# Cross-covariance attention: the V side moved later, with V loads and stores alternating in the closing part

## The chip, the cores and the metric

The kernel runs on one core of one Trainium2 chip. The metric is device time in microseconds (us) of one execution, taken as the median over runs. Times inside an execution are counted from the start of the profiled span.

## The reference

Q, K and V are float32 of shape (8, 12, 512, 64): 96 heads of 512 rows by 64 columns. Each column of Q and K is divided by its norm over the 512 rows. The attention matrix is 64 x 64 for each head, not 512 x 512:

```python
attn = np.einsum('bhnd,bhne->bhde', Q_norm, K_norm)
attn = np.exp(attn - np.max(attn, axis=-1, keepdims=True))
attn = attn / (np.sum(attn, axis=-1, keepdims=True) + 1e-10)
return np.einsum('bhnd,bhde->bhne', V, attn)
```

So every byte of Q, K and V is read once and the output, as large as V, is written once.

## The kernel before

Four heads make a unit, so there are 24 units (U = 24, numbers 0 to 23). One unit of Q, K, V or output is 512 KB and travels as one DMA. All DMAs are issued by SP in program order: 24 loads each of Q, K and V, and 24 stores, the last of them split into two halves of 256 KB. The order of work on every engine is written out by hand (`manual_schedule`), and each engine takes its instructions strictly in that order.

The attention side of a unit s runs as follows. DVE casts Q and K to bf16 (`cast_q` line 80, `cast_k` line 83). PE forms the gram matrices in 32 matmuls (`grams`, line 96). DVE reads the squared norms off the diagonals (`norms`, line 111), POOL raises them to the power -0.5 (line 116) and scales K's half of the gram (`scale_k`, line 121), which ACT had copied out of PSUM (`keep_kq`, line 104). PE transposes (`logits`, line 127), DVE scales by Q's norm (`scale_q`, line 131), ACT takes the exponential (`exps`, line 135), and DVE divides by the sum (`normalise`, lines 139 to 143). The finished matrix of unit u goes into a buffer of `abuf`, chosen by u modulo the number of buffers; PE and ACT then put a second copy into its lower half (`doubled`, lines 160 and 161). The zeros of these buffers are written once, at the start, by POOL (line 194).

The V side of a unit is a cast to bf16 (`cast_v`, line 87, on ACT in the loop and on DVE in the closing part), eight transposes on PE and their copy to SBUF on ACT (`vtrans`, lines 153 and 155), and sixteen matmuls with two copies out of PSUM (`outs`, lines 171 and 175). In the loop both copies are ACT's. In the closing part, from the unit after n1 on, one of them is DVE's.

One loop runs over s = 0 to 23. `outs_by(s)` says how many units of V have their outputs by the end of step s. In step s, SP gets the loads of Q and K of unit s + 3, then loads of V up to unit n1 + 3 and stores up to unit n1 - 4, where n1 = outs_by(s). Before the change outs_by(s) = (s - 2) * 10 // 11, so that n1 is 19 in the last step: the loop leaves the outputs of five units, one V load and eight stores to the closing part.

Buffers limit how early things can start: five for Q and for K, six for the float32 V (`vp`), four for the bf16 V, three for the transposed V, ten for the outputs, two PSUM tiles each for the grams (`ps_g`, which the closing part's `vtrans` also uses) and for the outputs.

The closing part begins after the loop with `logits(last)`. There the attention of the last unit is completed, and the outputs of the remaining units follow.

Of the kernel before, what the change touches and what calls it, by code (L numbers as in the profile page):

```python
# [23 lines left out]
def kernel(  # L24
# [7 lines left out]
    nc = tc.nc  # L32
    B, H, N, _ = Q.shape
    assert N == MV * R and Q.shape[3] == D
    U = B * H // HU
# [21 lines left out]

    def outs_by(s):

        return max(0, (s - 2) * 10 // 11)  # L60


    qf, kf, vf, vb, qkb, gram, nsq, rq, kqs, sl, ex, vt, so, kq = ({} for _ in range(14))
# [7 lines left out]
    def load_v(u):  # L71
        vf[u] = vp.tile([128, SV, TP * 2 * D], F32, name="vf")
        nc.sync.dma_start(out=vf[u], in_=Vf[u])

    def store(u, g=slice(0, SV)):
        nc.sync.dma_start(out=Of[u][:, g], in_=so[u][:, g].rearrange("p s t d -> p s (t d)"))
# [8 lines left out]
    def cast_v(u, copy=nc.scalar.copy):  # L85
        w = vb[u] = vbp.tile([128, SV, TP, 2 * D], BF16, name="vb")
        copy(w.rearrange("p s t d -> p s (t d)"), vf[u])  # L87
# [37 lines left out]
    def logits(u):  # L125
        for h in range(HU):
            nc.tensor.transpose(lg[:, h, :], kqs[u][D:, h, :], ident[D:, D:])  # L127

    def scale_q(u):
        s = sl[u] = small.tile([D, HU, D], F32, name="sl")  # L130
        nc.vector.tensor_tensor(out=s, in0=lg, in1=rq[u][0:D, :, None].to_broadcast([D, HU, D]), op=ALU.mult)  # L131
# [5 lines left out]
    def normalise(u):  # L137
        s = small.tile([D, HU], F32, name="esum")
        nc.vector.reduce_sum(out=s, in_=ex[u], axis=AX.X)  # L139
        ri = small.tile([D, HU], F32, name="rinv")  # L140
        nc.vector.reciprocal(ri, s)
        a = abuf[u % len(abuf)]
        nc.vector.tensor_tensor(out=a[0:D, :, 0, :], in0=ex[u], in1=ri[:, :, None].to_broadcast([D, HU, D]), op=ALU.mult)  # L143

    def vtrans(u, spare=False):

        if not spare:
            ps = ps_v.tile([128, SV, TP, 128], BF16, name="vps")
        else:
            ps = ps_g.tile([128, 2, 512], F32, name="gram")[:, 0].bitcast(BF16).rearrange("p (s t c) -> p s t c", s=SV, t=TP)  # L150
        for g in range(SV):
            for t in range(TP):
                nc.tensor.transpose(ps[:, g, t, :], vb[u][:, g, t, :], identb)  # L153
        w = vt[u] = vtp.tile([128, SV, TP, 128], BF16, name="vt")
        nc.scalar.copy(w, ps)  # L155

    def doubled(u):

        a = abuf[u % len(abuf)]
        nc.tensor.matmul(dup[D:], identb[0:D, 0:D], a[0:D, :, 0, :], tile_position=(0, D))  # L160
        nc.scalar.copy(a[D:, :, 1, :], dup[D:])  # L161

    def outs(u, copies=(nc.scalar.copy, nc.scalar.copy)):
        s = so[u] = sop.tile([128, SV, TP, 2 * D], F32, name="so")
        a = abuf[u % len(abuf)]
        for g in range(SV):
            po = ps_o.tile([128, TP, 2 * D], F32, name="po")
            for t in range(TP):
                for x in range(2):
                    rows = slice(MV * x, MV * (x + 1))  # L170
                    nc.tensor.matmul(  # L171
                        po[rows, t, :], vt[u][:, g, t, rows],
                        a[:, 2 * g + x].rearrange("p a d -> p (a d)"), tile_position=(0, MV * x),
                    )
            copies[g](s[:, g], po)  # L175
# [13 lines left out]
    mhalf = const.tile([128, HU], F32, name="mhalf")  # L189
    nc.gpsimd.memset(mhalf, -0.5)  # L190
    abuf = []
    for i in range(9):
        a = const.tile([128, HU, 2, D], BF16, name=f"ab{i}")
        nc.gpsimd.memset(a, 0.0)
        abuf.append(a)

    def on(f, u):
        if 0 <= u < U:
            f(u)
# [5 lines left out]
    nv, nst, nt = 2, 0, 0  # L205
    for s in range(U):
        n0, n1 = outs_by(s - 1), outs_by(s)
        on(load_qk, s + LOAD_AHEAD)
        while nv < min(U, n1 + 4):
            load_v(nv)  # L210
            nv += 1
        while nst < n1 - 3:
            store(nst)
            nst += 1
        new = range(nt, n1 + 1) if s >= 1 else ()
        for v in new:
            cast_v(v)
        on(cast_q, s + 1)
        on(normalise, s - 2)
        on(grams, s)  # L220
        on(norms, s)
        on(keep_kq, s)
        on(scale_k, s)
        on(logits, s - 1)
        on(scale_q, s - 1)
        on(exps, s - 1)
        on(cast_k, s + 1)
        for v in range(n0, n1):
            outs(v)
        on(doubled, s - 2)  # L230
        for v in new:
            vtrans(v)
            nt = v + 1
    for u in range(nv, U):
        load_v(u)
    for u in range(nst, U):
        if u >= n1:
            break
        store(u)
        nst += 1  # L240


    last = U - 1
    both = (nc.scalar.copy, nc.vector.tensor_copy)
    logits(last)
    cast_v(n1 + 1, nc.vector.tensor_copy)
    normalise(last - 1)
    scale_q(last)
    exps(last)
    outs(n1)  # L250
    store(n1)
    vtrans(n1 + 1, True)
    doubled(last - 1)
    normalise(last)
    doubled(last)
    cast_v(n1 + 2, nc.vector.tensor_copy)
    for u in range(n1 + 1, U):
        if u + 1 < U:
            vtrans(u + 1, True)
        if u + 2 < U:  # L260
            cast_v(u + 2, nc.vector.tensor_copy)
        outs(u, both)
        if u < last:
            store(u)
    for g in range(SV):
        store(last, slice(g, g + 1))

# [29 lines left out]
```

## Time and profile before

| what | value |
|---|---|
| median of 7 runs | 136.63 us (135.52 to 137.26) |
| the profiled execution's own time | 137.26 us |
| its span | 135.5 us |
| moved by the hardware DMA queue | 50.34 MB, mean of all queues 373 GB/s |
| PE busy | 87.5 us (65%) |
| DVE busy | 89.8 us (66%) |
| ACT busy | 96.0 us (71%) |
| POOL busy | 64.3 us (47%) |
| mean granted TensorE clock | 0.836 |

The span runs from the first to the last instruction; the execution's own time is 1.76 us longer. The profiled execution is the slowest of the seven, 0.63 us above their median. The busy times are means over a loop and a closing part which differ much, so no engine's share tells by itself what sets the end.

### The profile page before, as it was taken

The page shows a single profiled execution, that of the slowest core. Times are in us where ns is not written, and L with a number is a line of the kernel's source. Part 1 is how long each engine was busy: PE and PEld are TensorE (multiplying, and loading weights), DVE is VectorE, ACT ScalarE, POOL GpSimd, SP SyncE. Part 2 cuts the span into 40 slices and gives each one's busy share as a digit, 9 for nine tenths or more (in the row PEclk, how much of TensorE's full clock was granted, in tenths as well). Part 3 has the DMA queues.
Part 4 walks back from the last instruction along what each step waited for, and adds up shares of the span by engine and source line. Part 5 has one row for each costly group of instructions (what it writes and reads, how often), then busy time and mean ns, then how long its engine had stood idle before and what let it go on. Part 6 is the DMA issues. An engine that isn't in the chain of part 4 may idle for free.

```text
span 135.5 us, 3877 instructions
## 1 busy us (share of the span) xinstructions
PE 87.5 (65%) x1464; PEld 69.4 (51%) x1464; DVE 89.8 (66%) x344; ACT 96.0 (71%) x161; POOL 64.3 (47%) x65
## 2 busy tenths in 40 slices
PE   0056854397677696785965595868955388976940
PEld 0046733275455474564853484647744266654730
DVE  0755662989988888878684859776482766843540
ACT  3002730549999999999997397999978488986760
POOL 8705641478678638564276337642642426510000
PEclk9999999999999959999599559995599955555595
DMA  4999999999999999999999999999999999997475
GB/s 125 377 391 389 387 387 388 386 384 386 385 386 386 406 405 395 405 397 397 402 396 402 406 391 400 403 400 404 402 400 402 408 409 399 406 402 287 161 269 221
DMA packets 26146, 50.58 MB, mean 373 GB/s; under 512 B 1552, under 2 KB 1552, under 8 KB 26128
## 3 DMA queue, kind: packets, MB, share of 16 engines
q1 hardware_dynamic: 26128, 50.34, 98.5%
q8 instruction: 11, 0.18, 0.5%
q14 instruction: 7, 0.06, 0.1%
HBM read 37.75 MB, written 12.58 MB: 371 GB/s over the span
## 4 chain that ended last, share of the span: by engine, by line
DMA 54%; ACT 14%; PE 12%; DVE 12%; issue 3%; SPq 1%; ACTq 0%; DVEq 0%
DMA qf<-in_Q_dram 54%; DVE scr L111 4%; PE gram L96 4%; ACT so L175 4%; ACT vt L155 4%; PE po L171 3%; PE gram L153 3%; ACT vb L87 2%; DVE qkb L80 2%; ACT ab L161 2%; ACT ex L135 1%; PE vps L153 1%; DVE sl L131 1%; ACT kq L104 1%; DVE so L175 1%
## 5 line engine op out<-in xcount | busy, mean ns | idle before, releaser
L116 POOL TENSOR_TENSOR rq<-nsq,mhalf 128x4 f32<-128x4 f32 x24 | 44.3, 1847 | 51.6 <-DVE nsq L111 39.0
L96 PE MATMUL gram<-qkb 64*128 64x128 bf16 x768 | 35.1, 261 | 9.6 <-DVE qkb L83 9.6
L96 PEld LDWEIGHTS <-qkb 64*128 64x128 bf16 x768 | 29.9, 117 | 19.6 <-DVE qkb L83 17.1
L80 DVE CAST qkb<-qf 128x1024 bf16<-128x1024 f32 x24 | 18.1, 752 | 22.8 <-DMA qf<-in_Q_dram 22.7
L104 ACT COPY kq<-gram 64x256 f32<-64x256 f32 x24 | 8.8, 368 | 26.5 <-DVE nsq L111 26.2
L111 DVE CUSTOM_DVE_ANT_0 scr<-gram,ident 128x128 f32<-128x128 f32 x96 | 21.9, 279 | 5.7 <-PE gram L96 5.7
L175 ACT COPY so<-po 128x512 f32<-128x512 f32 x44 | 23.8, 589 | 0.7 <-PE po L171 0.2
L171 PE MATMUL po<-ab,vt 128*64 128x128 bf16 x384 | 19.0, 255 | 6.5 <-ACT vt L155 5.6
L87 ACT CAST vb<-vf 128x1024 bf16<-128x1024 f32 x20 | 21.0, 1048 | 2.7 <-DMA vf<-in_V_dram 2.7
L153 PEld LDWEIGHTS <-vb 128*128 128x128 bf16 x192 | 14.0, 116 | 16.0 <-ACT kq L104 9.4
L155 ACT COPY vt<-vps 128x1024 bf16<-128x1024 bf16 x20 | 20.2, 1012 | 0.7 <-PE vps L153 0.3
L171 PEld LDWEIGHTS <-vt 128*64 128x64 bf16 x384 | 14.7, 131 | 10.6 <-ACT vt L155 8.9
L127 PE MATMUL lgdup<-ident,kqs 64*64 64x64 f32 x96 | 12.2, 264 | 9.8 <-POOL kqs L121 5.1
L160 PE MATMUL lgdup<-ab,identb 64*64 64x256 bf16 x24 | 7.5, 314 | 15.6 <-DVE sl L131 14.3
L83 DVE CAST qkb<-kf 128x1024 bf16<-128x1024 f32 x24 | 16.2, 675 | 0.0
L153 PE MATMUL vps<-identb,vb 128*128 128x128 bf16 x160 | 15.0, 249 | 1.8 <-ACT vb L87 1.2
L121 POOL TENSOR_TENSOR kqs<-kq,rq 64x256 f32<-64x256 f32 x24 | 14.8, 617 | 2.4 <-POOL rq L116 0.6
L127 PEld LDWEIGHTS lgdup<-ident,kqs 64*64 64x64 f32 x96 | 8.4, 136 | 12.4 <-POOL kqs L121 9.4
L131 DVE TENSOR_TENSOR sl<-lgdup,rq 64x256 f32<-64x256 f32 x24 | 9.9, 413 | 3.1 <-PE lgdup L127 2.4
L139 DVE TENSOR_REDUCE esum<-ex 64x4 f32<-64x256 f32 x24 | 9.8, 406 | 3.3 <-ACT ex L135 3.2
L143 DVE TENSOR_TENSOR ab<-ex,rinv 64x256 bf16<-64x256 f32 x24 | 10.7, 445 | 0.8
L135 ACT ACTIVATE ex<-sl 64x256 f32<-64x256 f32 x24 | 10.0, 417 | 0.9 <-DVE sl L131 0.3
(18 smaller groups left out, 43.2 us busy)
## 6 DMA issues: line engine op xcount, KB each, us to landing
qf<-in_Q_dram SPq DMA_DIRECT2D x24, 512.0 KB, 10.4
kf<-in_K_dram SPq DMA_DIRECT2D x24, 512.0 KB, 10.4
vf<-in_V_dram SPq DMA_DIRECT2D x24, 512.0 KB, 10.3
out_dram<-so SPq DMA_DIRECT2D x23, 512.0 KB, 10.2
out_dram<-so SPq DMA_DIRECT2D x2, 256.0 KB, 2.8
```

What stands on the lines that cost most here:

```text
L80: nc.vector.tensor_copy(qkb[u][:, :, :, 0:D], qf[u].rearrange("p s (t d) -> p s t d", d=D))
L83: nc.vector.tensor_copy(qkb[u][:, :, :, D:], kf[u].rearrange("p s (t d) -> p s t d", d=D))
L87: copy(w.rearrange("p s t d -> p s (t d)"), vf[u])
L96: nc.tensor.matmul(g[:, c, 2 * D * p:2 * D * (p + 1)], x, x, start=(t == 0), stop=(t == R - 1), tile_position=(MV * c, 0),)
L111: nc.vector.tensor_tensor_reduce(out=scr, in0=gram[u][:, h % 2, 2 * D * (h // 2):2 * D * (h // 2 + 1)], in1=ident, scale=1.0, scalar=1e-20 ...
L116: nc.gpsimd.tensor_tensor(out=r, in0=n2, in1=mhalf, op=ALU.pow)
L121: nc.gpsimd.tensor_tensor(out=kk[D:], in0=kq[u][D:], in1=rq[u][D:, :, None].to_broadcast([D, HU, D]), op=ALU.mult,)
L127: nc.tensor.transpose(lg[:, h, :], kqs[u][D:, h, :], ident[D:, D:])
L153: nc.tensor.transpose(ps[:, g, t, :], vb[u][:, g, t, :], identb)
L155: nc.scalar.copy(w, ps)
L171: nc.tensor.matmul(po[rows, t, :], vt[u][:, g, t, rows], a[:, 2 * g + x].rearrange("p a d -> p (a d)"), tile_position=(0, MV * x),)
L175: copies[g](s[:, g], po)
```

## The change

The V side is set to 4/5 of a unit for each step. The last step then has n1 = 16 where it had 19, and the closing part has the outputs of eight units in place of five. The number of `abuf` buffers, and of the memsets that fill them at the start, goes from 9 to 12. In the closing part each `move(u)` issues the load of V of unit u + 4 and the store of unit u - 3. Outputs and transposes of V stand on PE between `logits(last)` and `doubled(last)`. The remaining stores come at the end, in order, the last one in two halves as before.

```diff
     def outs_by(s):
-        return max(0, (s - 2) * 10 // 11)
+        return max(0, (s - 2) * 4 // 5)
...
-    for i in range(9):
+    for i in range(12):
...
-    for u in range(nv, U):
-        load_v(u)
-    for u in range(nst, U):
-        if u >= n1:
-            break
-        store(u)
-        nst += 1
-
     last = U - 1
     both = (nc.scalar.copy, nc.vector.tensor_copy)
+
+    def v_ahead(u):
+        if u + 1 < U:
+            vtrans(u + 1, True)
+
+    def cast_ahead(u):
+        if u < U:
+            cast_v(u, nc.vector.tensor_copy)
+
+    def move(u):
+        on(load_v, u + 4)
+        store(u - 3)
+
+    move(n1)
+    cast_ahead(n1 + 1)
+    normalise(last - 1)
     logits(last)
-    cast_v(n1 + 1, nc.vector.tensor_copy)
-    normalise(last - 1)
     scale_q(last)
     exps(last)
     outs(n1)
-    store(n1)
-    vtrans(n1 + 1, True)
+    v_ahead(n1)
+    cast_ahead(n1 + 2)
+    normalise(last)
     doubled(last - 1)
-    normalise(last)
+    move(n1 + 1)
+    v_ahead(n1 + 1)
+    cast_ahead(n1 + 3)
+    outs(n1 + 1, both)
     doubled(last)
-    cast_v(n1 + 2, nc.vector.tensor_copy)
-    for u in range(n1 + 1, U):
-        if u + 1 < U:
-            vtrans(u + 1, True)
-        if u + 2 < U:
-            cast_v(u + 2, nc.vector.tensor_copy)
+    for u in range(n1 + 2, U):
+        move(u)
+        v_ahead(u)
+        cast_ahead(u + 2)
         outs(u, both)
-        if u < last:
-            store(u)
+    for u in range(U - 3, last):
+        store(u)
     for g in range(SV):
         store(last, slice(g, g + 1))
```

The order of SP's queue changes with it. Ahead of the loads of Q and K of unit 23 there stood V loads up to unit 18 and stores up to unit 11; now there stand V loads up to unit 16 and stores up to unit 9. Behind the last V load there are the stores of units 16 to 23 in both kernels.

## The prediction

> **What bounds the kernel now.** I read the slices first, then the stretches, then SP's timeline of the stores, then the closing part engine by engine. Rows of the page in 40 slices of 3.39 us:
>
> ```profile
> PEclk9999999999999959999599559995599955555595
> DMA  4999999999999999999999999999999999997475
> GB/s 125 377 391 389 387 387 388 386 384 386 385 386 386 406 405 395 405 397 397 402 396 402 406 391 400 403 400 404 402 400 402 408 409 399 406 402 287 161 269 221
> ```
>
> Transfers are the bound for 36 slices; only the last four have holes. The same in the view by stretches (busy us of PE, PEld, DVE, ACT, POOL, then granted clock, DMA share, GB/s):
>
> ```profile
> 113.40:122.00 8.60, 7.51 (x93) 5.87 (x92) 5.04 (x20) 7.60 (x14) 3.24 (x4) 0.50 1.05 404
> 122.00:126.00 4.00, 2.80 (x29) 1.90 (x30) 1.05 (x3) 2.78 (x5) 0.00 (x0) 0.50 0.67 253
> 126.00:132.00 6.00, 4.07 (x64) 3.27 (x62) 3.28 (x5) 4.06 (x6) 0.00 (x0) 0.77 0.60 226
> 132.00:135.50 3.50, 0.00 (x0) 0.00 (x0) 0.00 (x0) 0.00 (x0) 0.00 (x0) 0.52 0.59 224
> ```
>
> From 122 us on the queue runs half empty: stores wait for outputs. Line 76 of SP's timeline has store 18 issued at 118.51 us, 19 at 121.75, 20 at 126.67, 21 at 128.63, and the last ones from 130.42 on. Those waits, and the timeline of the closing part (start us, us, engine, line):
>
> ```profile
> SPq L76 <- DVE so L175: 7.1, 3, 4.5
> ...
> 109.45 0.69 DVE L80 CAST qkb<-qf 128x1024 bf16<-128x1024 f32 x1 [1.71 <-DMA qf<-in_Q_dram]
> 116.74 0.67 DVE L87 CAST vb<-vf 128x1024 bf16<-128x1024 f32 x1
> 120.25 0.42 ACT L135 ACTIVATE ex<-sl 64x256 f32<-64x256 f32 x1 [0.33 <-DVE sl L131]
> 125.80 1.03 PE L153 MATMUL gram<-identb,vb 128*128 128x128 bf16 x8
> 126.77 1.06 PE L171 MATMUL po<-ab,vt 128*64 128x128 bf16 x16
> 128.73 0.64 PE L171 MATMUL po<-ab,vt 128*64 128x128 bf16 x16
> 128.89 1.01 ACT L155 COPY vt<-gram 128x1024 bf16<-128x1024 bf16 x1 [0.46 <-PE gram L153]
> 130.89 0.69 DVE L175 COPY so<-po 128x512 f32<-128x512 f32 x1 [0.79 <-PE po L171]
> ```
>
> The last attention starts when Q of unit 23 lands (109.45), its exponential ends at 120.67, and five units of outputs are squeezed behind it, each at 1.96 us of PE at half clock (125.80 and 127.76 begin two such units). The last copy ends at 131.58; the span ends 3.9 us later (store issue, 2.8 us to landing, the end). So: transfers bound the loop, PE at half clock bounds the closing part, and there is a gap between them.
>
> **The change part by part.** *Loop.* Ahead of Q of unit 23 two V loads and two stores fewer stand in SP's queue. SP issues at one transfer per 1.30 us there (109.49, 110.79, 112.09, 113.40), so Q 23 lands 4 x 1.30 = 5.2 us earlier, at about 104.2. The total of transfers is unchanged.
>
> Engines must follow faster. A step with V takes at least 4.3 us (ACT's pairs of line 175 start at 30.10, 34.40, 38.71, 43.02, at full clock), or at half clock PE's sum 1.89 + 0.63 + 1.06 + 0.41 + 1.03 = 5.0. Steps come in fives, four with V and one without (PE 2.9 at half clock, DVE about 3.7): 4.2 on average at full, 4.8 at half clock, against (4 x 4 + 2) / 5 x 1.30 = 4.7 of transfers. The average is covered, the order not quite: Q 22 lands 2.6 us after Q 21, and Q 23 only 5.2 after that. Two steps need 8.6 to 10.0 where arrivals take 7.8, so the last casts lag by 0.8 to 2.2. I take 1.3: cast of Q 23 at 105.5. From there to the end of the exponential it was 11.2 us; the chain (grams, norms, POOL's 1.65 and 0.61, transposes) keeps its links, and V's instructions leave the last step. End of the exponential: 116.7, 4 us earlier; 115.3 at full clock (grams 0.8, transposes 0.4, logits 0.2 shorter). I take 116.
>
> *Closing part.* ACT from there has, in its order: two copies of unit 16 (1.07), transposed V 17 (1.01), the second copy of attention 22 (0.37), transposed V 18 (1.01), one copy of 17 (0.60), the second copy of 23 (0.37), then five transposed V at 1.03 and six copies at 0.61 with the gaps: 13.3 us in all, 129.3. DVE has 0.67 + 0.69 a unit and lies beside it. PE has 1.03 + 1.06 a unit at half clock, 0.62 + 0.64 at full: 2.1 is more than ACT's 1.64, 1.3 is less. The clock decides which engine sets the pace.
>
> Row and rule: in the closing part of before, PE alternates transposes and outputs without a gap from 123.85 on, and its clock went from half to full at 128.8, after 4.9 us (1.06 at 126.77, 0.64 at 128.73). The Trainium skill ("TensorE: Matmul & The Clock Gate", Part 4, PE-mode transpose) says that transposes don't count as PE-busy for the gate, which speaks against a closing part with seven units of them. By the rule the clock stays at half: eight outputs and seven transposes of units, 8 x 1.06 + 7 x 1.03 + 0.8 for the second copies = 16.5 us from about 115, the last copy at 132.2. By the row it is released some 5 us into the gapless work, near 120, and until then PE and ACT are about level (units 16 to 18 done at 122 by either sum): loss 0.5, last copy at 129.8. The trace has such a stretch of exactly this mix, so I take the row.
>
> *Stores.* Compute end 129.8 + 3.9 = 133.7. Transfers have their own floor: store 19 (issued 121.75, 5.6 to landing) landed at 127.35; four units remained. A lone stream of stores runs at 385 to 389 GB/s here, 1.35 us each: 132.75, and 0.95 from landing to the end: 133.7 as well. As neither covers the other wholly I add 0.3: span 134.0.
>
> *SP.* Stores and V loads alternate at the end. The load of V 23 takes the buffer of V 17 (six of `vp`), so it waits for DVE's cast of V 17, which `cast_ahead` puts behind the norms of unit 23: it was at 116.74 for the same place, 7.3 after the cast of Q 23, so at 112.8 to 113.5. SP would otherwise issue it near 110.7 to 112. Behind it stand all remaining stores, the first of which has no data before 117. Eight transfers are under way, 10 us of work, so I cost it at 0; it would cost its whole delay beyond that cover. *Early end of the queue:* store 15 waits for outputs in the last V step, at about 110, near its slot (109.4); same cover, 0. *DVE* casts V 17 and 18 ahead of `scale_q` and `normalise` of unit 23: 0.67 each beside POOL's 2.3 us and ACT's exponential, 0. *PE* has outputs of 16 queued behind `logits(last)`, so it stands idle while POOL works in the last step: that is inside the 116.
>
> *Twelve buffers.* Nine memsets end at 5.86 (4.22 us, 0.47 each); three more end 1.4 later. The first cast of Q took 2.15 us where its mean is 0.752 and ended 0.54 after them, so it ends up to 1.4 later:
>
> ```profile
> 1.64 4.22 POOL L194 MEMSET ab<- 128x512 bf16 x9
> 4.25 2.15 DVE L80 CAST qkb<-qf 128x1024 bf16<-128x1024 f32 x1 [4.25 <-DMA qf<-in_Q_dram]
> 22.78 0.69 DVE L80 CAST qkb<-qf 128x1024 bf16<-128x1024 f32 x1 [3.41 <-DMA qf<-in_Q_dram]
> ```
>
> DVE waits for Q for 3.41 us before 22.78 and 1.31 at 15.81; these take the 1.4 up, and no load is held since five buffers stand ready. Cost 0; without that cover 1.4. More buffers gain nothing: unit 23 normalises where unit 14 lay with nine, and its outputs are long done.
>
> *Sum.* Span 135.5 - 1.5 = 134.0. The profiled execution adds 1.76 and lies 0.63 above the median: 134.0 + 1.76 - 0.63 = 135.1.
>
> **The rivals.** *The earlier start is eaten (no change).* The last copy stays near 131.5: a lag of 2.2 in the loop, 0.7 more of half clock. For it: PE is at half from 108.4 to 128.8 in before, and every step of the loop is then over its transfers' time. Against it: a PE without gaps was released four times in the loop (50.5, 67.3, 80.8, 97.9). Median 136.6, 136.0 to 137.2.
>
> *Half clock to the end (slower).* PE at half clock from step 20 on: exponential at 117.6, outputs from 116.4, 16.5 us of PE and a copy of 0.7: 133.6, span 137.5, median 138.6. It decides from a last copy later than 131.6. For it: the rule above, and that three units more now come after the attention, 3 x 2.1 = 6.3 us at half clock against an attention 4 us earlier. Against: the row at 128.73.
>
> *Transfers bind harder.* If fewer stores among the loads cost rate (loads alone 389 GB/s from 23 to 47 us, 400 with one store in four), 56 transfers of the loop at 0.2% to 1% more give up to 0.7: 135.8. *Nothing happens* is excluded: the order of SP's queue is different.
>
> **How the numbers follow.** Main case 0.66, its own range 133.9 to 135.9: below, a full clock from the start (compute end 128.8) with a quicker tail of stores; above, the lag of 2.2. No change 0.20, slower 0.14. A difference under 0.5% (0.68 us) can't be told from none in this kernel. The range 133.9 to 137.3 leaves out the half-clock case and little else. Faster 0.66, same 0.20, slower 0.14.
>
> **What would show it.** Right: Q 23 landing near 104, the last exponential ending at 115 to 117, outputs at 0.64 us on PE by 121, stores issued every 1.3 to 1.7 us at the end, holes in the last four DMA slices shrunk to under half. Wrong: casts of Q 22 and 23 ended by PE and not by DMA with over 2 us of lag; outputs at 1.06 to the end; an empty queue while SP waits for the cast of V 17.

## The result and the profile after

The changed kernel takes 135.17 us (median of 24 runs, 134.69 to 136.23) against 136.37 for the kernel before (61 runs): a ratio of 0.9914, with a 95% interval of 0.9897 to 0.9932. The profiled execution took 135.25 us with a span of 133.4. Its slices, to be laid beside those of before:

```profile
PEclk9999985569999955999955999555599996589965
DMA  4999999999999999999999999999999999999980
GB/s 151 369 383 397 389 389 384 387 384 391 382 387 386 408 391 397 403 403 394 402 407 390 401 401 405 403 401 406 393 402 395 405 410 398 408 405 388 395 333 36
```

The hole in the last four slices is gone: transfers run at 388 and 395 GB/s where there were 287 and 161. In their place stands one slice with next to nothing in it, the very last. By stretches (busy us of PE, PEld, DVE, ACT, POOL; granted clock, DMA share, GB/s):

```profile
113.00:122.00 9.00, 8.32 (x125) 6.61 (x122) 6.42 (x13) 8.47 (x14) 0.00 (x0) 0.73 1.05 403
122.00:126.00 4.00, 2.81 (x63) 2.37 (x60) 2.52 (x4) 3.53 (x7) 0.00 (x0) 1.00 1.03 393
126.00:130.00 4.00, 0.06 (x3) 0.00 (x0) 0.69 (x1) 0.46 (x1) 0.00 (x0) 0.76 0.91 349
130.00:133.40 3.40, 0.00 (x0) 0.00 (x0) 0.00 (x0) 0.00 (x0) 0.00 (x0) 0.50 0.10 39
```

All engines are done before 127 us (the last copy ends at 126.79) and transfers go on by themselves to the end. The timeline of the closing part (start us, us, engine, line):

```profile
103.49 0.69 DVE L80 CAST qkb<-qf 128x1024 bf16<-128x1024 f32 x1 [1.20 <-DMA qf<-in_Q_dram]
113.30 0.42 ACT L135 ACTIVATE ex<-sl 64x256 f32<-64x256 f32 x1 [2.46 <-DVE sl L131]
...
112.08 0.63 PE L127 MATMUL lgdup<-ident,kqs 64*64 64x64 f32 x4 [2.08 <-POOL kqs L121]
114.95 1.03 PE L153 MATMUL gram<-identb,vb 128*128 128x128 bf16 x8
115.91 1.06 PE L171 MATMUL po<-ab,vt 128*64 128x128 bf16 x16
118.05 0.64 PE L171 MATMUL po<-ab,vt 128*64 128x128 bf16 x16
...
126.10 0.69 DVE L175 COPY so<-po 128x512 f32<-128x512 f32 x1 [0.73 <-DMA out_dram<-so]
...
SPq L300 <- DMA out_dram<-so: 5.0, 2, 3.8
```

The cast of Q 23 starts at 103.49 (109.45 before), the last exponential ends at 113.72 (120.67), PE is at full clock by 118.05 (128.73), and the last copy ends at 126.79 (131.58). From the last copy to the end of the span it was 3.9 us; now it is 6.6. The last row, from SP's waits, says the same: at the end SP waits 5.0 us in all for stores to land, where the last work of an engine used to be followed by a store of 2.8 us. So in these two executions the outputs came 4.8 us earlier and the span ends 2.1 us earlier. The rest went into waiting for transfers. The medians differ by 1.2 us and not by 2.1, because the profiled execution of before is 0.9 us above the median of its 61 runs and that of the change 0.1 above its own.

### The profile page after: what moved, and what is told of

Its sections match the earlier page's. It is cut to its first block, busy times and chain, and to the rows that moved or that the text cites. A ratio compares the mean times of both kernels' runs of the same rounds, so it can differ in the third digit from the quotient of the medians.

```text
span 133.4 us, 3882 instructions
## 1 busy us (share of the span) xinstructions
PE 84.2 (63%) x1464; PEld 66.7 (50%) x1464; DVE 94.7 (71%) x350; ACT 91.2 (68%) x155; POOL 66.0 (49%) x68
## 2 busy tenths in 40 slices
DMA packets 26146, 50.58 MB, mean 379 GB/s; under 512 B 1552, under 2 KB 1552, under 8 KB 26128
## 4 chain that ended last, share of the span: by engine, by line
DMA 50%; DVE 13%; PE 11%; ACT 11%; issue 4%; POOL 3%; SPq 1%; POOLq 1%; DVEq 0%; ACTq 0%
DMA qf<-in_Q_dram 46%; DVE scr L111 5%; DMA out_dram<-so 5%; ACT so L175 4%; PE gram L96 4%; DVE qkb L80 3%; ACT vt L155 2%; PE po L171 2%; POOL rq L116 2%; PE gram L153 2%; ACT vb L87 2%; DVE sl L131 2%; DVE esum L139 1%; PE lgdup L160 1%; ACT ex L135 1%
## 5 line engine op out<-in xcount | busy, mean ns | idle before, releaser
L96 PE MATMUL gram<-qkb 64*128 64x128 bf16 x768 | 33.6, 254 | 12.0 <-DVE qkb L83 12.0
L96 PEld LDWEIGHTS <-qkb 64*128 64x128 bf16 x768 | 28.4, 113 | 22.7 <-DVE qkb L83 20.8
L80 DVE CAST qkb<-qf 128x1024 bf16<-128x1024 f32 x24 | 19.6, 817 | 15.8 <-DMA qf<-in_Q_dram 15.8
L175 ACT COPY so<-po 128x512 f32<-128x512 f32 x41 | 22.5, 591 | 0.9 <-PE po L171 0.5
L127 PE MATMUL lgdup<-ident,kqs 64*64 64x64 f32 x96 | 12.0, 260 | 13.3 <-POOL kqs L121 7.8
L87 ACT CAST vb<-vf 128x1024 bf16<-128x1024 f32 x17 | 17.8, 1047 | 1.7 <-DMA vf<-in_V_dram 1.6
L155 ACT COPY vt<-vps 128x1024 bf16<-128x1024 bf16 x17 | 17.2, 1012 | 0.4
L153 PEld LDWEIGHTS <-vb 128*128 128x128 bf16 x192 | 12.9, 110 | 8.8 <-ACT kq L104 4.5
L153 PE MATMUL vps<-identb,vb 128*128 128x128 bf16 x136 | 12.2, 241 | 0.4
L143 DVE TENSOR_TENSOR ab<-ex,rinv 64x256 bf16<-64x256 f32 x24 | 10.5, 438 | 0.8
```

The costliest lines, as they stand in the source:

```text
L80: nc.vector.tensor_copy(qkb[u][:, :, :, 0:D], qf[u].rearrange("p s (t d) -> p s t d", d=D))
L96: nc.tensor.matmul(g[:, c, 2 * D * p:2 * D * (p + 1)], x, x, start=(t == 0), stop=(t == R - 1), tile_position=(MV * c, 0),)
```

## The experiments

Theory A: the lower rate of the V side starts the last attention earlier, that brings the outputs in front of the transfers, and the transfers then set the end. Theory B: the new order of the closing part does it. Later two theories on that order were added, C and D. All ratios are to the kernel before on the same chip, with 95% intervals; on these chips before took 136.1 to 136.7, so ratios are to be compared and not medians. The last copy and the span come from one profiled execution of each kernel, which can lie well off the median (the rate alone was profiled at 136.68, the closing part alone at 135.90, the change with the line back at 134.71). Executions also differ in when the last attention is done: in the five kernels that have the loop of the change at its rate, the last exponential ended between 113.72 and 115.70. Where the order of the closing part is judged, the time from the last exponential to the last copy is therefore given too.

| kernel | median us | ratio | last copy ends | span |
|---|---|---|---|---|
| before | 136.37 | 1 | 131.58 | 135.5 |
| the change | 135.17 | 0.9914 (0.9897 to 0.9932) | 126.79 | 133.4 |
| rate alone | 135.51 | 0.9942 (0.9918 to 0.9966) | 129.41 | 134.9 |
| closing part alone | 135.01 | 0.9908 (0.9875 to 0.9940) | 130.39 | 134.1 |
| rate 7/8 | 135.70 | 0.9940 (0.9917 to 0.9963) | 130.6 | 134.3 |
| rate 3/4 | 135.30 | 0.9932 (0.9907 to 0.9956) | 126.65 | 133.7 |
| one line of before moved | 135.15 | 0.9908 (0.9869 to 0.9948) | 129.98 | 133.7 |
| the change, that line back | 135.25 | 0.9927 (0.9903 to 0.9952) | 128.76 | 132.9 |
| both copies on ACT | 135.64 | 0.9937 (0.9915 to 0.9960) | 130.37 | 134.4 |

**The rate alone.** V load 23 is put behind the cast that frees its buffer; the rest of the closing part is that of before.

```diff
-        return max(0, (s - 2) * 10 // 11)
+        return max(0, (s - 2) * 4 // 5)
...
-    for u in range(nv, U):
+    last_v = n1 + 7
+    for u in range(nv, last_v):
         load_v(u)
...
     cast_v(n1 + 1, nc.vector.tensor_copy)
+    for u in range(last_v, U):
+        load_v(u)
     normalise(last - 1)
```

> V side at 4/5 of the rate and 9 buffers for the attention, but the closing part in the order of before: V loads 20 to 22 together, then stores 13 to 15, V load 23 behind the cast of V 17 that frees its buffer, no outputs of V on PE between the last two second copies. Theory A (the rate fills the transfer queue, which then sets the end): as the changed kernel, 135.2 us, 134.8 to 135.6, hole in the last DMA slices gone. Theory B (the order of the closing part brings the gain): as before, about 136.4. If both count: in between, near 135.8.

Measured 135.51, within A's interval, but the last copy ended 2.6 us later than in the change. The DMA share between 118 and 126 us was 0.80 to 0.95, so the hole had shrunk and moved, not gone. The rate by itself is worth something, 0.3% to 0.8% by its interval; the interval of the change, 0.7% to 1.0%, overlaps it.

**The closing part alone.** The changed kernel with the old rate.

```diff
-        return max(0, (s - 2) * 4 // 5)
+        return max(0, (s - 2) * 10 // 11)
```

> The closing part and the 12 buffers of the change with the old rate 10/11, so that five units are left for the closing part. Theory A: as before, 136.4 us, 136.0 to 136.8, with the hole in the DMA slices from 122 us on. Theory B: as the changed kernel, 135.2. A gain of 0.2 to 0.4 would be the two items of V that PE and ACT do ahead of the last second copy.

Measured 135.01. Theory A fails here: with the old rate the last attention was no earlier than before (its exponential ended at 121.03), the hole in the transfers was still there (0.53 of DMA share from 124 to 126 us), and yet the whole gain stood. The last copy came 1.2 us earlier all the same. With only one V load left in the closing part at this rate, SP's queue is that of before too, so the alternation of loads and stores is not what did it. What differs is the order on PE, ACT and DVE. PE of before, between the two second copies of the attention (line 160):

```profile
121.93 0.42 PE L160 MATMUL lgdup<-ab,identb 64*64 64x256 bf16 x1
123.55 0.37 PE L160 MATMUL lgdup<-ab,identb 64*64 64x256 bf16 x1 [1.20 <-ACT ab L161]
123.85 1.03 PE L153 MATMUL gram<-identb,vb 128*128 128x128 bf16 x8
```

Both go through one PSUM tile, so the second waits for ACT to read the first, and ACT had the copy of a transposed V ahead of it. PE stood for 1.20 us at half clock. Theory C: that gap is the cause, directly and by the later release of the clock. Theory D: something else in the closing part.

**One line of before moved.** No other change to the kernel before.

```diff
     normalise(last)
-    doubled(last)
     cast_v(n1 + 2, nc.vector.tensor_copy)
...
         outs(u, both)
+        if u == n1 + 1:
+            doubled(last)
         if u < last:
```

> The kernel before with one line moved: the second copy of the last attention comes after the outputs of unit n1 + 1 instead of ahead of the transposes that precede them. Theory C (the order gains by taking away PE's wait of 1.2 us for ACT between the two second copies, after which PE has no gap and its clock is released earlier): most of the gain of the closing part alone, 135.0 to 135.5, PE at full clock by about 126 us instead of 128.8. Theory D (what helped the closing part alone was something else in it, as the buffers or the earlier casts): as before, 136.3.

Measured 135.15, as good as the whole change. PE in that kernel, and its last copy:

```profile
121.74 0.42 PE L160 MATMUL lgdup<-ab,identb 64*64 64x256 bf16 x1
123.17 1.06 PE L171 MATMUL po<-ab,vt 128*64 128x128 bf16 x16
124.16 0.42 PE L160 MATMUL lgdup<-ab,identb 64*64 64x256 bf16 x1
125.48 0.66 PE L171 MATMUL po<-ab,vt 128*64 128x128 bf16 x16
...
129.29 0.69 DVE L175 COPY so<-po 128x512 f32<-128x512 f32 x1 [0.73 <-PE po L171]
```

No wait stands at the second row of line 160 any more (the third row here), the outputs are at full clock at 125.48 where they were still at half at 126.77, and the last copy ends 1.6 us earlier from an exponential that ended only 0.2 us earlier (120.45). Theory C holds. From the exponential to the last copy it took 9.5 us in place of 10.9. How much of these 1.4 us is the gap itself and how much the earlier release of the clock, 125.6 in place of 128.7, was not told apart.

**The same line put back in the changed kernel.**

```diff
     doubled(last - 1)
+    doubled(last)
     move(n1 + 1)
     v_ahead(n1 + 1)
     cast_ahead(n1 + 3)
     outs(n1 + 1, both)
-    doubled(last)
```

> The changed kernel with the second copy of the last attention put straight behind that of the one before it, as in the kernel before. Theory C: PE waits 1.2 us for ACT again and keeps half clock some 2 us longer, so the last output copy comes 1.5 to 2.5 us later, near 129; transfers cover most of it, so the time rises by 0 to 0.4: 135.2 to 135.6. Theory D: no change in the last copy either.

Measured 135.25, and the last copy 2.0 us later than in the change. The wait is back, and PE is at full clock from 120.7 in place of 117.8:

```profile
116.70 0.37 PE L160 MATMUL lgdup<-ab,identb 64*64 64x256 bf16 x1 [1.20 <-ACT ab L161]
```

The last exponential was 0.5 us later in this execution; from it to the last copy it took 14.6 us in place of 13.1. So the order is worth 1.5 us of outputs here too, and nothing in the time, since transfers cover it.

**Other rates.** The changed kernel with `* 7 // 8` and with `* 3 // 4`.

> The changed kernel with 7/8 in place of 4/5: six units left for the closing part, and two transfers instead of four fewer ahead of Q of unit 23. Theory A: the last attention starts 2.6 us earlier than before and one unit more (1.3 to 2.1 us) comes after it, so the last copy is 0.5 to 1.3 us earlier than before and outputs still set the end: 135.2 to 135.9. If transfers set the end already: 135.2. If the order of the closing part is what counts: 135.2 as well, told apart by e2.

> The changed kernel with 3/4 in place of 4/5: nine units left for the closing part. Theory A: transfers already set the end at 4/5 with some 3 us of cover for the outputs, so nothing more is gained: 135.2, 134.8 to 135.7. A rival in which the end follows the last output copy by 3.9 us expects the last copy about as late or 1 us later (one unit more at 1.4 us, attention 1.3 to 2.6 us earlier), with a time that moves with it one for one.

At 3/4 the last copy ended at 126.65, about where it does at 4/5, and the time was the same: nothing to gain below. At 7/8 the time fell in A's range, but that range hardly tells it from the others: all the intervals overlap.

**Both copies on ACT.** A test of how much cover the outputs have after the change.

```diff
-    both = (nc.scalar.copy, nc.vector.tensor_copy)
+    both = (nc.scalar.copy, nc.scalar.copy)
```

> The changed kernel with both output copies of every unit on ACT in the closing part, which adds some 0.48 us of ACT to each of seven units, 3.3 us in all. Theory A (transfers set the end after the change, outputs have about 3 us of cover): the last copy near 130 and the time up by 0 to 0.6, 135.2 to 135.8. The rival in which the end follows the last copy by a fixed time: up by 3.3, 138.5.

The last row of ACT there (four copies in one row), and for the other end the last copy at rate 3/4:

```profile
128.04 2.33 ACT L175 COPY so<-po 128x512 f32<-128x512 f32 x4
```

```profile
125.96 0.69 DVE L175 COPY so<-po 128x512 f32<-128x512 f32 x1 [0.79 <-PE po L171]
```

The last copy is 3.6 us later than in the change (1.1 of it because the exponential was) and the time 0.3 (by the ratios) to 0.5 us longer (by the medians), with intervals that overlap. A fixed distance from the last copy to the end is excluded: it was 7.1 us at rate 3/4, 6.6 in the change, 4.0 here, and 3.7 to 3.9 where the last copy came latest.

**No transposes in the closing part.** `vtrans` with `spare` returns the transposed V of the unit before, in the kernel before and in the changed one.

```diff
     def vtrans(u, spare=False):
+        if spare:
+            vt[u] = vt[u - 1]
+            return
```

> The kernel before without the transposes of V and their copies in the closing part (four units: they use the transposed V of an earlier unit, so that part of the computation is left out). Theory A (outputs, not transfers, set the end before): the last copy 4 us or more earlier, the hole in the last DMA slices gone, and the time at the floor of the transfers, 134.9 to 135.3. If transfers set the end already: as before, 136.3.

> The changed kernel without the transposes of V and their copies in the closing part (seven units: they use the transposed V of an earlier unit, so that part of the computation is left out). Theory A (transfers set the end after): the last copy several us earlier and the time unchanged, 135.2 within 0.3. The rival in which outputs still set it: down by the same several us.

In the kernel before it gives 135.15, a ratio of 0.9893 (0.9871 to 0.9915): taking closing work away from before is worth what the change is worth. The time is as theory A has it, but two of its signs missed. In the profiled execution, the slowest of the 19 (136.74), the last copy ended at 129.42, 2.2 us earlier and not 4 or more, and the hole was shallower but still there (a DMA share of 0.72 to 0.82 from 124 to 129 us). In the changed kernel it gives 135.37 (0.9911, 0.9883 to 0.9939): nothing more. One half of that expectation missed. The last copy did not come several us earlier but 1.7 later, at 128.47:

```profile
120.47 1.07 PE L174 MATMUL po<-ab,vt 128*64 128x128 bf16 x16 [0.67 <-ACT so L178]
122.21 1.07 PE L174 MATMUL po<-ab,vt 128*64 128x128 bf16 x16 [0.67 <-ACT so L178]
125.69 1.07 PE L174 MATMUL po<-ab,vt 128*64 128x128 bf16 x16 [0.67 <-ACT so L178]
```

With the transposes gone PE stands still for 0.67 us in a unit and keeps half clock to the end (line 174 is line 171 moved by the edit). The last exponential ended at 115.70 here, 2.0 us later than in the change, and the loop ahead of it is the same; so the lateness is not the edit's. From there to the last copy it took 12.8 us in place of 13.1: seven units of transposes less gained 0.3 us. This run bounds the cover from the other side only: outputs 1.7 us later cost no more than 0.2.

**Nine buffers** in the changed kernel.

> The changed kernel with 9 instead of 12 buffers for the attention. All theories: the first cast of Q ends 1.4 us earlier, and the time stays, 135.2 within 0.3, since DVE waits for Q afterwards anyway. A rival in which the later start is carried through would gain 1.0 to 1.4: 133.8 to 134.2.

Measured 135.31, a ratio of 0.9916 (0.9885 to 0.9948): no difference in the time. The first cast of Q ended at 6.39 us in place of 7.80, 1.4 earlier as expected, and later waits took that up.

**The transfers alone**, in the changed kernel's order, on one queue and on two. Nothing is computed: each store sends the unit of V that was loaded, and V has ten buffers.

> The changed kernel's transfers alone, in its order and on its queue: all loads and stores, and nothing computed (each store sends the unit of V that was loaded, so the attention and the outputs are left out; V has ten buffers). Theory A (transfers bound the changed kernel from end to end): 135.0 within 0.4. If computing still costs something in it, the time is lower by that: 133 to 134.5.

> The same transfers alone (nothing computed) with the odd units issued by ACT instead of SP. If the floor is the rate of the 16 DMA engines: as the transfers alone on one queue, within 0.5. If the slowest engines' lag at the end belongs to the one queue, 1 to 2 us less.

Measured 133.33 (0.9793, 0.9733 to 0.9854) and 132.46 (0.9727, 0.9677 to 0.9777), four runs each. Theory A's 135.0 fails: the changed kernel is 1.8 us above its own transfers. The end by single us (the last two columns are DMA share and GB/s), first of the changed kernel and then of its transfers alone:

```profile
128.00:129.00 1.00, 0.00 (x0) 0.00 (x0) 0.00 (x0) 0.00 (x0) 0.00 (x0) 0.52 1.03 393
129.00:130.00 1.00, 0.00 (x0) 0.00 (x0) 0.00 (x0) 0.00 (x0) 0.00 (x0) 0.50 0.56 213
130.00:131.00 1.00, 0.00 (x0) 0.00 (x0) 0.00 (x0) 0.00 (x0) 0.00 (x0) 0.50 0.25 94
131.00:132.00 1.00, 0.00 (x0) 0.00 (x0) 0.00 (x0) 0.00 (x0) 0.00 (x0) 0.50 0.09 35
```

```profile
128.00:129.00 1.00, 0.00 (x0) 1.00 1.04 401
129.00:130.00 1.00, 0.00 (x0) 1.00 0.45 170
130.00:131.00 1.00, 0.00 (x0) 1.00 0.00 0
```

Both run at the full share up to 129 us. Alone, the transfers stop together; in the kernel the share falls off over more than two us. The trace holds 16 completion marks for each DMA (1552 for 97 DMAs), one for each of 16 parts, and these show what lags; the landing time that the profile gives is the last of them. The first part of the last store landed at 129.4 us in the changed kernel and at 129.3 alone, its last part at 132.5 and at 130.4. So the last part lagged by 3.1 us behind the first in one and by 1.1 in the other.

The lag grew in steps, and the steps fall on transfers of instructions, which the profile counts on the same 16 DMA engines. The rows of their queues, first for the changed kernel and then for its transfers alone (packets, MB, share of 16 engines):

```profile
q8 instruction: 11, 0.18, 0.5%
q14 instruction: 7, 0.06, 0.1%
```

```profile
q14 instruction: 1, 0.01, 0.0%
```

In the changed kernel the lag went from 1.5 us to 2.0, 3.0, 3.6 and 4.5, each time with the first transfer whose last part landed after the end of a 16 KB packet of q8 (these began at 19.69, 33.13, 99.64 and 109.77 us and took 0.95 to 1.11 us each); between 10 and 118 us it made no other step over 0.3. The other packets moved other parts: the lags of all 16 parts together went from 5 us at 18 us to 28 at 118, and alone only from 6.5 to 8.4. The kernel before has two such steps of 1.6 us, with the packets at 18.42 and 99.64. Alone, without packets of 16 KB, the lag stayed between 0.8 and 1.2. That instructions hold up some of the parts is read from this timing; the traces don't name the engine of a packet, and no run changed the instructions alone.

**The last parts of the last stores.** They also show why one line brought what the whole change brought. When the last part landed (us, one profiled execution each):

| kernel | store 19 | store 20 | store 21 | store 22 | end of store 23 |
|---|---|---|---|---|---|
| before | 127.3 | 129.5 | 131.4 | 133.2 | 134.5 |
| the change | 127.4 | 128.7 | 129.9 | 131.2 | 132.5 |
| one line of before moved | 127.4 | 128.7 | 130.0 | 131.4 | 132.8 |

With the change these parts land every 1.29 us to the end (half that for each half of store 23), as in the ten us before: they don't run out of work. In before, three steps took 2.1, 2.0 and 1.8 us, together 2.0 more than three times 1.29, and the spans differ by 2.1. Store 19 landed at the same time in both, so the hole that the mean share shows from 122 us on (0.95 to 0.28) cost the lagging parts nothing until 127; they were still busy with earlier stores. Only stores 20 to 22 came too late for them. With the one line moved the mean share still drops to 0.47 from 124 to 126 us, and the lagging parts lose under 0.2 us. So the floor that the change and the one line reach is the lagging parts' own queue of work, and a mean over 16 engines can't show when it is reached.

On two queues the transfers alone are another 0.9 us faster, with runs of 132.36 to 132.52 against 132.85 to 133.42 though the intervals of the ratios overlap. The expectation had within 0.5 or 1 to 2 us less, and 0.9 fits neither. The kernel itself was not tried that way.

No version that computes everything beats the changed kernel clearly: with it, six stand between 135.01 and 135.31.

## Why the prediction was right, and where its steps were off

The time, 135.1 forecast and 135.17 measured, is right by the term it named: the span ends at the floor of the transfers, forecast at 133.7 and measured at 133.4. That floor was counted from the landing of store 19, at 127.35, with 1.35 us for each store after it and 0.95 at the end. Store 19 landed at 127.4 again, the stores took 1.29 us each, and 0.9 followed. As it was counted from the landing of the last part, it already contained the lag.

That the number is within 0.1 us is in part luck. The span was put at 134.0, 0.6 too high (0.3 of it added for the meeting of two limits, which was not needed). The 0.63 taken off because the profiled execution of before was the slowest of seven made up for it; that of the change was 0.1 above its median. "Compute end 129.8 + 3.9 = 133.7", the other half of the sum, does not hold: the last copy ended 3.0 us earlier than forecast.

*Loop.* Q 23 was forecast to land at 104.2 and its cast to lag by 1.3; the cast began at 103.49 and DVE waited for Q there, so no lag. The 4.3 us a step were ACT's, and DVE's casts can come closer: 95.07 and 98.44 were the two casts ahead of it. PE was at full clock from 97.3 to 111.0, so the chain from cast to exponential took 10.2 us, where 11.2 had been read and 10.5 was taken, and the exponential ended at 113.72 instead of 116. That is earlier than the sign "115 to 117"; in the four other executions with this loop it ended at 114.2 to 115.7.

*ACT's tail* was 13.3 us forecast and 12.7 measured (113.72 to the end of ACT's last copy at 126.46).

*The clock.* The row was the right thing to follow, and not the remark in the Trainium skill ("TensorE: Matmul & The Clock Gate", Part 4, PE-mode transpose) that transposes don't count as PE-busy for the gate. About half of PE's time in the 3.41 us ahead of 117.8 were transposes, and the clock was released all the same. In a stretch that alternates transposes and outputs PE was released at 117.8, some 6 us after it began at 112.08, in the manner of 123.85 to 128.7 before. But "some 5 us into the gapless work" is not the whole rule: PE of before also ran without a gap from 112.35 to 118.24 and stayed at half clock. In both traces every stretch at one clock, the first and the last aside, is 3.41 us long or a multiple of it. The clock rose only after such a step in which PE was busy for 91% or more by the trace's matmuls; the steps of 112.35 to 118.24 had 79% and 94% and did not suffice. So gapless work has to fill about a whole step, and when it began counts too. The run without transposes agrees: outputs alone, with gaps of 0.67 us, stayed at half clock.

*SP and the buffers.* The cast of V 17 came at 109.61, 3 us earlier than forecast, and did not hold V load 23: that was issued at 112.13, right after an earlier transfer had landed at 112.07. The queue stayed full: cost 0, as forecast. The three more memsets moved the end of the first cast from 6.40 to 7.80, the 1.4 us forecast, and the waits took them up:

```profile
1.64 5.60 POOL L194 MEMSET ab<- 128x512 bf16 x12
4.01 3.79 DVE L80 CAST qkb<-qf 128x1024 bf16<-128x1024 f32 x1 [4.01 <-DMA qf<-in_Q_dram]
22.00 0.69 DVE L80 CAST qkb<-qf 128x1024 bf16<-128x1024 f32 x1 [2.42 <-DMA qf<-in_Q_dram]
```

*The step that was missing.* The whole gain was credited to the earlier attention, and the order on PE between the last two second copies was given no term of its own. It has one: counted from the last exponential, 1.4 us of outputs in the kernel before (one line moved) and 1.5 in the changed one. The closing part or that one line brings the whole gain (0.9908 each), the rate alone 0.6% of the 0.9%, with overlapping intervals, and together they bring no more, because the time stops at the transfers while the outputs go on getting earlier. The prediction put both limits at the same 133.7 and so could not see how much of the change was spare. The rival with the half clock to the end did not come about even with the gap put back, where PE was released at 120.7.

## What to carry to other kernels

When an engine and a queue meet at the end of a kernel, work out both ends and look for the smallest edit that reaches the nearer one: here a single line, which moved a copy that waited for a PSUM tile away from the copy before it, brought what the reshaping of the whole schedule brought. In a closing part on PE, look for the gap first and the amount of work second, because here a gap cost its own length and held the clock down after it. Measure the transfers alone before calling them the floor, and follow when the last part of each store lands: a hole in the mean share cost nothing here as long as the lagging parts still had work.

## What was not expected of the hardware

Much less PE work gave hardly earlier outputs: without seven units of transposes PE stayed at half clock for want of gapless work, and the way from the last exponential to the last copy was shorter by only 0.3 us. The 16 parts of a transfer drifted apart by up to 4.5 us, in steps that fall on packets of instructions of about 1 us each. And the transfers alone on two queues took 132.46 us against 133.33 on one, in the same order.
